# A hybrid decoder trunk: queries, keys and gates by the seven-product form at the front of each mixer, kept in DRAM; other orders behind it

## The chip, the core and the metric

The kernel runs on one core of a Trainium2 chip. The metric is the device time of one execution in microseconds; of several runs the median counts. A core has TensorE (PE) for matrix products into PSUM, VectorE (DVE), ScalarE (ACT) and GpSimd (POOL) for elementwise work, SyncE (SP), which here issues transfers, and 16 DMA engines between DRAM and the core's memory (SBUF). Each engine takes its instructions in the order in which the program gives them, and waits on semaphores for the others.

## The reference, cut to what matters

Two layers over 512 positions of width 1024, one sequence:

```
x = x + 0.5 * swiglu(rms_norm(x, ffn1_norm[l]), ...)             # 1024 -> 2*2816 -> 1024
h = rms_norm(x, mix_norm[l])
proj = h @ w_in[l]
q, k, v, z, xbc, dt_raw, gate_sb, gate_ssm = split(proj)          # 512,512,512,1536,3584,24,1024,1024
y_sb = stick_breaking_attention(q, k, v) @ w_branch_sb[l]         # 4 heads x 128
y_ssm = mamba2_mixer(z, xbc, dt_raw, ...) @ w_branch_ssm[l]       # 8 groups, 24 heads x 64, state 128
merged = sigmoid(gate_sb) * y_sb + sigmoid(gate_ssm) * y_ssm
x = x + merged @ w_out[l]
x = x + 0.5 * swiglu(rms_norm(x, ffn2_norm[l]), ...)
```

The attention weight of a pair (t, s), s < t, is `exp(z - sp + within + cross)`: z is the scaled score, sp = softplus(z), and the other two are sums of -softplus over the positions between s and t. After the last layer comes one more RMSNorm. All is in fp32.

## The kernel before

**Products.** Tokens lie along the free axis (512), channels along the 128 partitions, so h is eight tiles of 128 x 512 ("blocks"). An fp32 product is made of three matmuls on numbers split into a high and a low part in fp32r: hi x hi, hi x lo, lo x hi (`mm3`, L363 to L365). So each operand needs a split first: the high part is a cast on ACT (weights L328, blocks of h L402, other tiles L452 or, with a factor, L454), the low part a subtraction on VectorE (L330, L403, L457, L459). A **plain block** makes 128 output channels: eight blocks of h, 24 matmuls of 512 columns (`dense`, `project`). The **seven** (`seven`, a Strassen form) makes four output blocks, two of each of two kinds, from seven products of 24 matmuls with 256 columns, on sums and differences of the two halves of h and of the weights; its results come in halves of 256 tokens.

**The order of the work.** One thread of Python makes the products in a fixed list; everything else is a generator put into a queue by `spawn(task, wait)`. `dense` calls `tick()` after every block of h (three matmuls), and the seven after every second: each tick takes every task one `yield` further. So `yield 3` is a distance of three ticks in the program, not a time, and the order on every engine is fixed when the program is built. A task that has to wait for another looks once a tick. Weights come in a list of units (L278 issues the load on SP), are split some units ahead, and the loads of DRAM copies and the spills stand in the same queue of SP.

**The norm's factor** `rs` is not known when the mixer begins: the first products are made on unscaled blocks of x times the gain, and the results are multiplied by `rs` afterwards (`scaled`, L593, or L595 with a factor). While that goes on, `scale_blocks` scales the blocks of x; one later product, called with `swap=True`, has the scaled blocks split anew (`swapped`, L402 and L403: the **swap**) for all that follow it.

**A mixer, before.** (1) Two sevens (`four_gates`) make the gates of output blocks 2 to 5, apply tanh and spill them to the DRAM array `gd`. (2) Plain blocks q0, k0 (PSUM tiles `pa`), q1, k1 (with the swap), q2, k2, then v by tokens, q3, k3. Each q and k is split from PSUM or scaled first (`qkv_parts`), and a head's `attention` is spawned after its k, 8 and 9 ticks later for the first two heads. (3) A list of steps (`group_steps`) mixes z, x, b, c blocks (with a four-tap convolution, `conv_block`, L1119 on ACT and three L1122 on VectorE), more gates, and the state-space scan of eight groups (`ssd_group`). Until all heads are done and dt is known, tanh is held back (`opened`), since ACT's table of functions has to be switched once (L222 for exp and ln, L1127 where it comes back). (4) Two branch products of attention, two first halves of the state-space branch products, then for each output block the second half, the merge with the gates, the next first half and the attention branch product two places ahead. (5) The output projection.

**One head's attention** (`attention`): for key blocks j = 3, 2, 1, 0 the scores go into `pa` (128 x 128, 256, 384, 512), then abs, exp, ln on ACT (L1021 to L1023), one instruction on VectorE (L1025), a causal mask on POOL, a split (`state` for the 128-wide term, `xs` for the others), sums of later blocks into `pa` by products with constant matrices (`nones` L1058, `ntri` L1060), exp, and a last split to weights.

## Time and profile before

| | us |
|---|---|
| median of three runs (2545.66 to 2546.43) | 2546.18 |
| the profiled execution | 2546.98 |
| its span, first to last instruction | 2545.3 |
| TensorE busy / VectorE / ACT / POOL | 2534.1 / 1796.7 / 1328.9 / 557.7 |
| TensorE waiting for ones, state, g, wlo | 1.1, 0.6, 0.2, 0.2 |

A row of the timeline has the start in us, the duration, the engine, the line of the kernel, the operation, out<-in by the program's names, shapes, and how many such instructions follow each other; in brackets stand the idle time before it and the engine and line that ended it. Starts of matmuls that follow each other give the pitch; a single duration is longer, since they overlap. Rows of waits give the sum, the count and the longest.

### The profile page before, as it was taken

What the parts mean: (1) busy time and instruction counts of PE and PEld (TensorE: products, weight loads), DVE (VectorE), ACT (ScalarE), POOL (GpSimd) and SP (SyncE); (2) the same over time, 40 slices, a digit from 0 to 9 for tenths busy, and PEclk for the clock granted to TensorE, in tenths of its full rate; (3) what the DMA queues carried; (4) which work ended last, traced back from release to release, by engine and by line L of the source; (5) the groups of instructions that cost most, each with busy time, mean ns of one, the idle gap of its engine ahead of it and who ended that gap; (6) DMA issues with size and microseconds to landing.
All of it is one profiled execution on the core that took longest, in us unless ns stands there. A gap on an engine that the chain in (4) does not pass through costs nothing.

```text
span 2545.3 us, 39422 instructions
## 1 busy us (share of the span) xinstructions
PE 2534.1 (100%) x15536; PEld 2293.7 (90%) x15536; DVE 1796.7 (71%) x2332; ACT 1328.9 (52%) x2193; POOL 557.7 (22%) x656
## 2 busy tenths in 40 slices
PE   9999999999999999999999999999999999999998
PEld 7898998889998889989899999988899988999997
DVE  8585886567765477758896768865777644876766
ACT  6353475666664264435563435656666643643434
POOL 0131300124443001313112222000244420122220
PEclk9999999999999999999999999999999999999999
DMA  4555574232233475656656556622333335755552
GB/s 153 157 155 159 161 199 128 75 120 89 102 100 96 145 211 151 172 151 165 180 126 177 148 166 172 199 98 78 115 102 102 100 105 163 194 142 169 145 163 83
DMA packets 112874, 357.35 MB, mean 140 GB/s; under 512 B 12784, under 2 KB 20400, under 8 KB 112688
## 3 DMA queue, kind: packets, MB, share of 16 engines
q1 hardware_dynamic: 96704, 299.13, 35.5%
q0 software_dynamic: 15120, 55.06, 12.1%
q8 instruction: 122, 2.00, 0.3%
q10 hardware_dynamic: 864, 0.64, 0.1%
q14 instruction: 64, 0.52, 0.1%
HBM read 342.10 MB, written 12.68 MB: 139 GB/s over the span
## 4 chain that ended last, share of the span: by engine, by line
PE 96%; DVE 2%; DMA 1%; issue 1%; ACT 1%; SPq 0%; POOL 0%; DVEq 0%; ACTq 0%; POOLq 0%
PE mm L363 26%; PE mm L364 26%; PE mm L365 26%; PE pa L364 4%; PE pa L363 4%; PE pa L365 4%; PE pa L1275 2%; PE pa L1278 1%; PE pt L1257 1%; PE pt L943 1%; PE pt L1253 1%; DVE wlo L330 1%; PE pa L943 0%; PE pa L1060 0%; DMA s<-in_wflat_dram 0%
## 5 line engine op out<-in xcount | busy, mean ns | idle before, releaser
L328 ACT CAST whi<-wraw 128x1024 fp32r<-128x1024 f32 (+3 forms) x433 | 427.8, 988 | 655.5 <-PE mm L365 438.1
L330 DVE TENSOR_TENSOR wlo<-wraw,whi 128x1024 fp32r<-128x1024 f32 (+3 forms) x433 | 533.3, 1232 | 229.4 <-ACT whi L328 228.6
L363 PE MATMUL mm<-hhi,whi 128*128 128x512 f32 (+1 forms) x1472 | 500.7, 340 | 0.0
L365 PE MATMUL mm<-hlo,whi 128*128 128x512 f32 (+1 forms) x1472 | 494.8, 336 | 0.0
L364 PE MATMUL mm<-hhi,wlo 128*128 128x512 f32 (+1 forms) x1472 | 494.5, 336 | 0.1
L365 PEld LDWEIGHTS mm<-hlo,whi 128*128 128x128 f32 x1472 | 276.0, 188 | 30.2
L363 PE MATMUL mm<-th,whi 128*128 128x256 f32 x1080 | 302.2, 280 | 0.0
L364 PEld LDWEIGHTS mm<-hhi,wlo 128*128 128x128 f32 x1472 | 276.6, 188 | 28.0 <-DVE wlo L330 0.6
L364 PE MATMUL mm<-th,wlo 128*128 128x256 f32 x1080 | 301.7, 279 | 0.2 <-DVE wlo L330 0.2
L365 PE MATMUL mm<-tl,whi 128*128 128x256 f32 x1080 | 301.3, 279 | 0.0
L363 PEld LDWEIGHTS mm<-hhi,whi 128*128 128x128 f32 x1472 | 276.4, 188 | 27.2
L330 DVE TENSOR_TENSOR wlo<-s,whi 128x1024 fp32r<-128x1024 f32 x180 | 257.2, 1441 | 34.0 <-ACT whi L328 30.4
L363 PE MATMUL mm<-act,whi 128*128 128x512 f32 (+1 forms) x710 | 273.9, 386 | 0.0
L364 PE MATMUL mm<-act,wlo 128*128 128x512 f32 (+1 forms) x710 | 273.7, 386 | 0.0
L365 PE MATMUL mm<-act,whi 128*128 128x512 f32 (+1 forms) x710 | 273.7, 385 | 0.0
L662 POOL TENSOR_TENSOR g<-g,rs 128x512 f32<-128x512 f32 x70 | 149.3, 2132 | 483.2 <-DVE g L641 453.7
L290 POOL DMA_DIRECT2D s<-in_wflat_dram x105 | 91.8, 899 | 712.2 <-DMA s<-in_wflat_dram 615.5
L328 ACT CAST whi<-s 128x1024 fp32r<-128x1024 f32 x180 | 188.7, 1048 | 61.2 <-PE mm L365 42.2
L365 PEld LDWEIGHTS mm<-tl,whi 128*128 128x128 f32 x1080 | 202.9, 188 | 0.0
L363 PEld LDWEIGHTS mm<-th,whi 128*128 128x128 f32 x1080 | 202.7, 188 | 0.0
L364 PEld LDWEIGHTS mm<-th,wlo 128*128 128x128 f32 x1080 | 202.2, 187 | 0.4 <-DVE wlo L330 0.4
L725 DVE SCALAR_TENSOR_TENSOR x<-mm,x 128x512 f32<-128x512 f32 x93 | 64.2, 690 | 190.8 <-PE mm L365 190.7
(313 smaller groups left out, 5304.0 us busy)
## 6 DMA issues: line engine op xcount, KB each, us to landing
wraw<-in_wflat_dram SPq DMA_DIRECT2D x321, 512.0 KB, 3.7
s<-in_wflat_dram POOLq DMA_DIRECT2D x105, 512.0 KB, 7.5
s<-in_wflat_dram SPq DMA_DIRECT2D x95, 512.0 KB, 5.2
wraw<-in_wflat_dram SPq DMA_DIRECT2D x88, 384.0 KB, 3.1
cumb<-cum_d SPq DMA_DIRECT2D x16, 768.0 KB, 5.0
xd<-x SPq DMA_DIRECT2D x16, 256.0 KB, 5.4
wraw<-in_wflat_dram SPq DMA_DIRECT2D x16, 256.0 KB, 3.3
x<-xd SPq DMA_DIRECT2D x16, 256.0 KB, 5.4
```

The costliest lines, as they stand in the source:

```text
L290: self.nc.gpsimd.dma_start(raw, self.stored(key[:-1] + (part,)), accum_op=ALU.add)
L328: nc.scalar.copy(hi[:, :n], raw[:, :n])
L330: nc.vector.tensor_tensor(lo[:, :n], raw[:, :n], hi[:, :n].bitcast(F32), op=ALU.subtract)
L363: mm(ps, a[0], b[0], start=start, stop=False, **kw)
L364: mm(ps, a[1], b[0], start=False, stop=False, **kw)
L365: mm(ps, a[0], b[1], start=False, stop=stop, **kw)
L662: eng.tensor_tensor(out, r, self.rs[:, cols].unsqueeze(1).to_broadcast([P, 2, SEQ // 2]), op=ALU.mult)
L725: self.nc.vector.scalar_tensor_tensor(x, pd, 0.5, x, op0=ALU.mult, op1=ALU.add)
L943: self.nc.tensor.transpose(pt[:, cs], src[:, cs], self.ident)
L1253: nc.tensor.matmul(cb, bt[:, span(c)], ct[:, span(c)], start=True, stop=True)
L1257: nc.tensor.matmul(pu, btok[:, c, :], xws[c].rearrange("p h d -> p (h d)"), start=True, stop=True)
L1275: nc.tensor.matmul(near[:, at:at + HD], decs[c][:, i, :], xdts[c][:, i, :], start=True, stop=True)
```

## The change

**At the front** a third seven is made, and the sevens' contents change (`four_blocks`): with j0 = 0 and 2 they make q and k of heads 0, 1 and 2, 3, with j0 = 4 the gates of output blocks 2 and 3. All twelve results are multiplied by `rs` and spilled to DRAM: q and k, in halves, to a new array `qd`, the gates after tanh to `gd`. The plain blocks behind the sevens are now the four gates of output blocks 4 and 5 (`rough_gate`): scaled and spilled without tanh (`rough`), which `finer` applies when they come back for the merge. The swap is in the fourth of them, and v follows at once.

**Attention** takes q and k from `qd` through three `raw` tiles (`reloaded`), and every head's task is spawned before the plain gates, with no distance. The weights' splits wait for the head before (`heads_out`). Its outputs lie in tiles of the block pool `x`, which stays open to the end of the merge.

**State-space groups.** The `y` tile of a group is opened by a task of its own (`direct`); `ssd_on` is released earlier and `y_busy` guards the tile, so that a group follows the one before at another distance; b and c of a group wait for `passed`.

**The merge.** Four first halves (AHEAD) instead of two come before the second halves, and the attention branch product in the loop is one place ahead, not two.

The diff, cut to its core:

```diff
+ROUGH = (4, 5)
+AHEAD = 4
...
-def qkv_order():
-    for h in range(SBH):
-        yield from (("q", h), ("k", h))
-        if h == SBH - 2:
-            for u in range(NT):
-                yield "v", u
+def opening_order():
+    for m in ROUGH:
+        yield from (("gs", m), ("gm", m))
+    for u in range(NT):
+        yield "v", u
...
-        if i + 2 < KB:
-            yield (layer, "bsb", MERGE_ORDER[i + 2]), SBH
+        if 0 < i < KB - 1:
+            yield (layer, "bsb", MERGE_ORDER[i + 1]), SBH
...
-    def four_gates(self, base, m, fp):
-        nc, half = self.nc, SEQ // 2
+    def four_blocks(self, base, fp):
+        nc, half, j0 = self.nc, SEQ // 2, base[-1]
         a, b = slice(0, half), slice(half, SEQ)
-        def squash(src, t, cols, scale):
+        def finish(src, t, cols, scale):
             while self.rs is None:
                 yield 1
             r = self.t(fp, [P, SEQ], "c", bufs=2) if t and cols is a else src
             self.normed_half(nc.vector, r, src, cols)
             yield 2
-            self.tables(False)
-            nc.scalar.activation(r, r, AF.Tanh, scale=scale)
-            yield 4
+            if j0 < SBH:
+                to, at = self.qd, 2 * j0
+            else:
+                to, at = self.gd, 2 * FRONT
+                self.tables(False)
+                nc.scalar.activation(r, r, AF.Tanh, scale=scale)
+                yield 4
             for j in range(2):
-                nc.sync.dma_start(self.gd[2 * (m + j) + t][:, cols], r[:, j * half:(j + 1) * half])
+                nc.sync.dma_start(to[at + 2 * j + t][:, cols], r[:, j * half:(j + 1) * half])
         def take(*how):
-            return lambda src: self.spawn(squash(src, *how))
+            return lambda src: self.spawn(finish(src, *how))
...
-    def qkv_parts(self, t, ps, normed, parts):
-        scale = P ** -0.5 if t == "q" else None
-        if normed:
-            two = self.pair(self.yt, ("yt", "yt"))
-            yield from self.split(two, ps, scale)
-            parts[t] = two
-            return
+    def reloaded(self, t, h, parts):
         r = yield from self.take("raw")
-        yield from self.scaled(r, ps, scale)
-        yield 2
+        self.nc.sync.dma_start(r, self.qd[2 * h + (t == "k")])
+        yield 7
         two = self.pair(self.yt, ("yt", "yt"))
-        yield from self.split(two, r)
+        yield from self.split(two, r, P ** -0.5 if t == "q" else -1.0)
         self.give("raw")
         parts[t] = two
...
+            while self.heads_out < h:
+                yield 1
...
+        self.heads_out = h + 1
         yield 2
-        two = self.pair(self.yo, ("ohi", "olo"))
+        two = self.pair(self.xp, ("x", "x"))
...
+        while kind != "x" and self.passed < i - 2:
+            yield 1
...
-            nc.gpsimd.tensor_tensor(heads(y[:, c, :]), x, wide(par[:, G_D + h0:G_D + h0 + HPG]), op=ALU.mult)
+        def direct(c0):
+            while self.y_busy not in (None, g):
+                yield 1
+            if self.y_busy is None:
+                self.y_busy = g
+                begun.append(self.t(mp, [P, NT, GW], "y", bufs=1))
+            for c in (c0, c0 + 1):
+                nc.gpsimd.tensor_tensor(heads(begun[0][:, c, :]), heads(xs[:, c, :]),
+                                        wide(par[:, G_D + h0:G_D + h0 + HPG]), op=ALU.mult)
+            begun.append(c0)
...
+    def rough(self, ps, r, spill):
+        yield 1
+        yield from self.scaled(r, ps)
+        yield 3
+        self.nc.sync.dma_start(spill, r)
+    def finer(self, *tiles):
+        yield 6
+        for r in tiles:
+            self.nc.scalar.activation(r, r, AF.Tanh, scale=0.5)
+            self.gated[r.name] = True
...
-        front = ExitStack()
-        fp = front.enter_context(tc.tile_pool(name=f"front{layer}", bufs=2, reuse_waits="tile"))
-        four = [self.four_gates((layer, 0, "pair", j), FRONT + j, fp) for j in range(0, EARLY - FRONT, 2)]
-        for part in four:
-            next(part)
-        for part in four:
-            for _ in part:
-                pass
-        self.close_t()
-        self.open_norm(self.x, gain)
-        self.hx = []
-        first = []
-        order = list(qkv_order())
-        for i in range(4):
-            while i == 3 and self.scaled_blocks < KB // 2:
-                self.tick()
-            first.append(self.project(layer, *order[i], swap=i == 3, aside=i < 2))
-        xd, self.xd = self.xd, None
-        front.close()
-        self.xpool.__exit__(None, None, None)
+        self.qd = self.t(self.dr, [2 * SBH, P, SEQ], "qd")
         with ExitStack() as mix:
             enter = mix.enter_context
+            gp = enter(tc.tile_pool(name=f"gates{layer}", bufs=2, reuse_waits="tile"))
+            def rough_gate(i):
+                t, m = order[i]
+                ps, _ = self.project(layer, t, m, swap=i == 3, aside=i < 2)
+                r = self.t(gp, [P, SEQ], t)
+                self.spawn(self.rough(ps, r, self.gd[2 * m + (t == "gm")]))
+            order = list(opening_order())
+            with tc.tile_pool(name=f"front{layer}", bufs=2, reuse_waits="tile") as fp:
+                four = [self.four_blocks((layer, 0, "pair", j), fp) for j in (0, 2, 4)]
+                for part in four[:2]:
+                    next(part)
+                for part in four:
+                    for _ in part:
+                        pass
+                self.close_t()
+                self.open_norm(self.x, gain)
+                self.hx = []
+                rough_gate(0)
+            xd, self.xd = self.xd, None
...
-                for i, (t, h) in enumerate(order):
-                    if t == "v":
-                        if h == 0:
-                            self.by_tokens(self.v_part, SEQ, layer, "v")
-                        continue
-                    ps, normed = first[i] if i < len(first) else self.project(layer, t, h)
-                    self.spawn(self.qkv_parts(t, ps, normed, parts[h]))
-                    if t == "k":
-                        self.spawn(self.attention(h, parts[h]), 8 + h if h < 2 else 0)
+                self.heads_out = 0
+                for h in range(SBH):
+                    for t in ("q", "k"):
+                        self.spawn(self.reloaded(t, h, parts[h]))
+                for h in range(SBH):
+                    self.spawn(self.attention(h, parts[h]))
+                for i in range(1, 4):
+                    while i == 3 and self.scaled_blocks < KB // 2:
+                        self.tick()
+                    rough_gate(i)
+                self.by_tokens(self.v_part, SEQ, layer, "v")
...
+                        if m not in ROUGH:
+                            self.gated[r.name] = True
+                    if m in ROUGH:
+                        self.spawn(self.finer(*gates[m]))
```

The order of the instructions moves with it. At the start of head 0's attention in layer 0, VectorE before (`cumb` is the scratch of the log terms, `state` and `xs` their low parts, `yt` splits of q and k, `wlo` of weights):

```order
L459 SCALAR_TENSOR_TENSOR yt_4261<-mm_4196,yt_4260 128x512
L330 TENSOR_TENSOR wlo_4258<-wraw_4119,whi_4257 128x1024
L1025 SCALAR_TENSOR_TENSOR cumb_4195<-pa_4284,cumb_4195 128x128
L1025 SCALAR_TENSOR_TENSOR cumb_4195<-pa_4291,cumb_4195 128x256
L457 TENSOR_TENSOR yt_4321<-mm_4251,yt_4320 128x512
L330 TENSOR_TENSOR wlo_4316<-wraw_4197,whi_4315 128x1024
L457 TENSOR_TENSOR state_4276<-cumb_4195,state_4275 128x128
L457 TENSOR_TENSOR xs_4278<-cumb_4195,xs_4277 128x256
```

and with the change (`hlo` is the swap, L593 a gate's scaling):

```order
L403 TENSOR_TENSOR hlo_4431<-x_86,hhi_4430 128x512
L1024 SCALAR_TENSOR_TENSOR cumb_4300<-pa_4393,cumb_4300 128x128
L459 SCALAR_TENSOR_TENSOR yt_4415<-raw_4362,yt_4414 128x512
L459 SCALAR_TENSOR_TENSOR yt_4418<-raw_4364,yt_4417 128x512
L459 SCALAR_TENSOR_TENSOR yt_4421<-raw_4366,yt_4420 128x512
L403 TENSOR_TENSOR hlo_4449<-x_87,hhi_4448 128x512
L1024 SCALAR_TENSOR_TENSOR cumb_4300<-pa_4400,cumb_4300 128x256
L593 TENSOR_TENSOR gs_4423<-mm_4350,rs_3669 128x512
L403 TENSOR_TENSOR hlo_4459<-x_88,hhi_4458 128x512
L330 TENSOR_TENSOR wlo_4435<-wraw_4302,whi_4434 128x1024
L403 TENSOR_TENSOR hlo_4469<-x_89,hhi_4468 128x512
L457 TENSOR_TENSOR state_4384<-cumb_4300,state_4383 128x128
```

Ahead of `state` now stand four splits of the swap, three of reloaded q and k, a gate's scaling and one weights' split, where one `yt` and one `wlo` stood behind the log terms. ACT at the same place, with the change, from the first abs of head 0 on:

```order
L1020 ACTIVATE cumb_4300<-pa_4400 128x256
L1021 ACTIVATE cumb_4300<-cumb_4300 128x256
L1022 ACTIVATE cumb_4300<-cumb_4300 128x256
L454 ACTIVATE yt_4414<-raw_4362 128x512
L454 ACTIVATE yt_4417<-raw_4364 128x512
L454 ACTIVATE yt_4420<-raw_4366 128x512
L402 CAST hhi_4430<-x_86 128x512
L328 CAST whi_4434<-wraw_4302 128x1024
L402 CAST hhi_4448<-x_87 128x512
L402 CAST hhi_4458<-x_88 128x512
L452 CAST state_4383<-cumb_4300 128x128
```

The three casts from `raw` stand between the ln and the first cast of the swap. And VectorE where ACT's table has been switched back after the last head, before:

```order
L330 TENSOR_TENSOR wlo_5375<-wraw_5262,whi_5374 128x1024
L1185 SCALAR_TENSOR_TENSOR z_4883<-raw_5393,z_4883 128x384
L1122 SCALAR_TENSOR_TENSOR cv_5385<-mm_5261,conv_4679,cv_5385 128x511
L1122 SCALAR_TENSOR_TENSOR cv_5388<-mm_5310,conv_4679,cv_5388 128x511
L1185 SCALAR_TENSOR_TENSOR z_4894<-raw_5400,z_4894 128x384
L1122 SCALAR_TENSOR_TENSOR cv_5385<-mm_5261,conv_4679,cv_5385 128x510
L1122 SCALAR_TENSOR_TENSOR cv_5388<-mm_5310,conv_4679,cv_5388 128x510
L1185 SCALAR_TENSOR_TENSOR z_4911<-raw_5408,z_4911 128x384
L1122 SCALAR_TENSOR_TENSOR cv_5385<-mm_5261,conv_4679,cv_5385 128x509
```

and with the change:

```order
L1189 SCALAR_TENSOR_TENSOR z_4935<-raw_5571,z_4935 128x384
L1124 SCALAR_TENSOR_TENSOR cv_5563<-mm_5342,conv_4760,cv_5563 128x511
L1124 SCALAR_TENSOR_TENSOR cv_5566<-mm_5405,conv_4760,cv_5566 128x511
L1189 SCALAR_TENSOR_TENSOR z_4948<-raw_5583,z_4948 128x384
L1124 SCALAR_TENSOR_TENSOR cv_5563<-mm_5342,conv_4760,cv_5563 128x510
L1124 SCALAR_TENSOR_TENSOR cv_5566<-mm_5405,conv_4760,cv_5566 128x510
L330 TENSOR_TENSOR wlo_5580<-wraw_5452,whi_5579 128x1024
L1189 SCALAR_TENSOR_TENSOR z_4971<-raw_5591,z_4971 128x384
L1124 SCALAR_TENSOR_TENSOR cv_5563<-mm_5342,conv_4760,cv_5563 128x509
```

The weights' split stood ahead of the first tap and is now behind the second pair of taps; a split of z leads. Between the last matmul of head 3 and the first that reuses the tile of the first of these two convolution blocks stood 57 matmuls of 512 columns and seven transposes on TensorE, and now 39 and seven.

## The prediction

> **What bounds the kernel now.** The page comes first: its busy times and, below them, the chain that ended last, by engine.

> ```profile
> span 2545.3 us, 39422 instructions
> PE 2534.1 (100%) x15536; PEld 2293.7 (90%) x15536; DVE 1796.7 (71%) x2332; ACT 1328.9 (52%) x2193; POOL 557.7 (22%) x656
> PE 96%; DVE 2%; DMA 1%; issue 1%; ACT 1%; SPq 0%; POOL 0%; DVEq 0%; ACTq 0%; POOLq 0%
> ```

> TensorE is the bound: 2534.1 of 2545.3 us, and no other engine is above 71%. So the time moves in two ways only: by TensorE's own work, and by stretches in which it stands still. How much standing still there is to win shows in the waits of TensorE (us in total, times, longest).

> ```profile
> PE pt L1566 <- DVE ones L518: 1.1, 1, 1.1
> PE pa L1058 <- DVE state L457: 0.6, 2, 0.3
> PE pt L773 <- ACT g L760: 0.2, 1, 0.2
> PE mm L364 <- DVE wlo L330: 0.2, 1, 0.2
> ```

> About 2 us in the whole program. Little can be gained, and every new wait counts in full. The second row matters: twice, once in each layer, TensorE waits for VectorE at the first weights of head 0.

> **TensorE's work: three sevens for two.** The starts of matmuls give the cost of the two forms, a plain block (24 matmuls of 512 columns) and a product of the seven (24 of 256):

> ```profile
> 390.92 0.40 PE L363 MATMUL pa<-hhi,whi 128*128 128x512 f32 x1
> 401.85 0.39 PE L363 MATMUL mm<-hhi,whi 128*128 128x512 f32 x1
> 365.48 0.28 PE L363 MATMUL pa<-th,whi 128*128 128x256 f32 x1
> 368.31 0.28 PE L363 MATMUL mm<-th,whi 128*128 128x256 f32 x1
> ```

> Between the first two starts lie two plain blocks: 10.93 us, 5.465 a block, 0.2277 a matmul. Between the last two lies one product: 2.83. A seven is 7 x 2.83 = 19.8 us, the four plain blocks that it stands for 21.9. Each layer makes one more block-of-four that way: 2 x 2.06 = **4.1 us less**. All else on TensorE is only reordered. The new casts, tanh and transfers lie beside TensorE's work wherever it does not wait for them: ACT has 48% free over the span and VectorE 29%. Without that cover the 16 reloads cost their two splits each, some 1.2 us.

> **Place A: the first head's attention meets the swap.** "Swap" is the moment at which the eight blocks of h are split again from their scaled values (one ACT and one VectorE instruction each). Before, two plain blocks stood between it and attention; now the three engines do both at once, and the order shows what stands ahead of `state`, the low part of head 0's first log term, for which TensorE waits. Before, in the same stretch:

> ```profile
> 428.59 0.50 PE L363 MATMUL mm<-whi,hhi 128*128 128x512 f32 x1
> 428.92 0.40 PE L364 MATMUL mm<-whi,hlo 128*128 128x512 f32 x1
> 429.39 0.22 PE L1058 MATMUL pa<-state,nones 128*128 128x128 f32 x1
> 429.92 0.33 PE L1058 MATMUL pa<-state,nones 128*128 128x128 f32 x1 [0.31 <-DVE state L457]
> 430.65 0.44 PE L363 MATMUL mm<-whi,hhi 128*128 128x512 f32 x1
> ```

> From 428.59 to 430.65 TensorE starts three matmuls of 512 columns (0.68) and six small ones (about 0.6): 0.8 us are lost a layer. The pieces' durations, on VectorE and then ACT:

> ```profile
> 411.28 1.22 DVE L330 TENSOR_TENSOR wlo<-wraw,whi 128x1024 fp32r<-128x1024 f32 x1
> 412.41 3.09 DVE L403 TENSOR_TENSOR hlo<-x,hhi 128x512 fp32r<-128x512 f32 x5
> 415.42 0.68 DVE L595 SCALAR_TENSOR_TENSOR raw<-pa,rs 128x512 f32<-128x512 f32 x1
> 418.35 1.89 DVE L457 TENSOR_TENSOR yt<-raw,yt 128x512 fp32r<-128x512 f32 x3
> 429.58 0.29 DVE L457 TENSOR_TENSOR state<-cumb,state 128x128 fp32r<-128x128 f32 x1
> 429.78 0.42 DVE L457 TENSOR_TENSOR xs<-cumb,xs 128x256 fp32r<-128x256 f32 x1
> 409.42 3.90 ACT L402 CAST hhi<-x 128x512 fp32r<-128x512 f32 x7
> 425.12 0.37 ACT L1021 ACTIVATE cumb<-pa 128x256 f32<-128x256 f32 x1
> 425.97 0.42 ACT L1023 ACTIVATE cumb<-cumb 128x256 f32<-128x256 f32 x1
> ```

> So a 512-column split takes VectorE 0.60 (five from 412.41 to 415.42) and a weights' split 1.13. Zero is the end of head 0's second score, 256 columns wide. From there TensorE has 27 matmuls of 512 columns before it needs `state`: 6.15 us. ACT needs a hand-over of about 0.2, then abs, exp and ln (425.12 to 426.39: 1.27), then by the new order three casts of reloaded queries and keys (0.6 each, 1.8) and one of the swap (0.56): 3.85. Only then can VectorE go on with `hlo`, and before `state` stand in its order: four `hlo` splits (2.4), two log terms (0.6 together), three `yt` splits (1.8), a gate's scaling (0.6), a weights' split (1.13), and `state` itself (0.29): 6.83. It is done at 10.7; **TensorE stands for 4.5**. Behind `state` come one more `hlo` (0.60) and `xs` (0.42), while TensorE has two small matmuls: 0.75 more. The next scores wait for an exp that stands behind a weights' cast on ACT; I take 0.6 (between 0 and one such cast, about 1), and 0.1 for refilling the pipeline (428.59 to 428.92 is 0.33 instead of 0.23). Sum 6.0; the bounds are 4.4 (the first wait alone) and 6.9 (the second cast in full, longer hand-overs).

> **Place B: the table switch after the last head.** ACT switches tables and catches up on the held tanh; VectorE starts the convolution taps of two blocks whose PSUM tiles TensorE wants back. Before:

> ```profile
> 535.48 0.28 PE L365 MATMUL pt<-dec,yt 128*128 128x128 f32 x1
> 549.37 0.39 PE L363 MATMUL mm<-hhi,whi 128*128 128x512 f32 x1
> 535.79 0.59 ACT L452 CAST ohi<-pt 128x512 fp32r<-128x512 f32 x1 [3.70 <-PE pt L365]
> 536.40 1.28 ACT L1127 ACT_TABLE_LOAD   x1
> 538.76 1.14 ACT L1127 ACTIVATE raw<-cv 128x512 f32<-128x512 f32 x2
> 541.25 1.44 ACT L1119 ACTIVATE cv<-mm,conv 128x512 f32<-128x512 f32 x2
> 542.59 1.76 ACT L1183 ACTIVATE raw<-z 128x384 f32<-128x384 f32 x4
> 543.14 0.56 DVE L1185 SCALAR_TENSOR_TENSOR z<-raw,z 128x384 f32<-128x384 f32 x1 [0.53 <-ACT raw L1183]
> 543.62 1.40 DVE L1122 SCALAR_TENSOR_TENSOR cv<-mm,conv,cv 128x511 f32<-128x511 f32 x2
> 544.93 0.55 DVE L1185 SCALAR_TENSOR_TENSOR z<-raw,z 128x384 f32<-128x384 f32 x1
> ```

> TensorE had 13.8 us of work (57 matmuls and seven transposes) between the head's last matmul and the one that reuses the tile: enough. Now the order has 39 matmuls and the transposes there: 39 x 0.2277 + 0.76 = 9.64. The chain against it: hand-over and cast 0.8, table 1.3, six held tanh at 0.53 (3.2, one more than before), two tap starts 1.34, the tanh of z 0.55: 7.18; then on VectorE by the new order z 0.48, two taps 1.31, z 0.47, two taps 1.31, a weights' split 1.13 (it stood ahead of the taps before, where VectorE was idle), z 0.47, and the third tap 0.74: 5.9. It ends at 13.1: **TensorE stands for 3.5**, 3.6 with the refill. Bounds: 2.9 (a tanh at 0.5, the tap's end overlapped) and 4.1 (one more hand-over of 0.2 at each of three changes of engine).

> Further on, in the first convolution blocks of group 1, an `xs` copy on ACT now stands behind held tanh, a weights' cast and a tap start just ahead of transposes: between 0 and 1.0; I take 0.4.

> **The sum.** A layer: 6.0 + 3.6 + 0.4 - 0.8 = 9.2. Two layers: +18.4. With -4.1: **+14.3**. The profiled execution took 2546.98 us (span 2545.3 and 1.7 around it), 0.8 above the median of the runs shown; 2546.98 + 14.3 = 2561.3, or **2560.5** on the median's footing. By the bounds a layer adds between 6.5 and 11.2: 2555 to 2564.5.

> What I cost at nothing: the spread of the state-space groups, the four leading first halves and the moved branch products. In the new order the values that TensorE needs there are ready, counted by the durations above, before it comes; the spills and reloads are queued on SP before weights that are used three or four units later, some 5 us each, while such a load lands in about 4:

> ```profile
> wraw<-in_wflat_dram SPq DMA_DIRECT2D x321, 512.0 KB, 3.7
> gs<-gd SPq DMA_DIRECT2D x12, 256.0 KB, 2.7
> ```

> Behind a reload that waits for a `raw` tile at place A stand only loads for the value blocks. If that cover is too short, the reload's 2.7 us is late in each layer.

> [...] The opening shows what standing still may cost beyond itself:

> ```profile
> 1.11 4.20 PE L1566 MATMUL pt<-ones 128*128 128x128 f32 x20 [1.11 <-DVE ones L518]
> 544.50 0.49 PE L943 MATMUL pt<-ident,bT 128*128 128x128 f32 x3
> 544.82 0.60 PE L943 MATMUL pt<-ident,cv 128*128 128x128 f32 x4
> ```

> At the start a 128-column matmul takes 0.21 (4.20 for 20), in full run 0.107 (0.32 for three): 2.1 us lost on the first 4.2. If a wait of 3.5 to 4.5 us put TensorE back into that slow pace, each of the four would cost 2.1 more. [...]

> **The rivals.**
> 1. *Only one of the two places stalls* (17%): the orders put it in the other engine's shadow, for example because at place B the held tanh run while TensorE still waits for ACT earlier. A alone: 2 x (6.0 + 0.4 - 0.8) - 4.1 = +7.1, 2553; B alone: 2 x (3.6 + 0.4) - 4.1 = +3.9, 2550. For it: place B has two steps whose handing over I only bound. Against: both chains are made of in-order instructions with durations that hardly vary.
> 2. *The elementwise work runs faster than its rows* (7%, the case of not slower): if ACT and VectorE did A's and B's instructions in half the time where their sources lie in SBUF, A would shrink to about 1.6 and B to about 0.5, and the sum to 2 x (2.1 - 0.8) - 4.1 = -1.5: 2544.7. It decides from VectorE chains of 2.3 us at A instead of 6.8. Against it: 412.41 and 418.35 are the same SBUF operands, at 0.60 each.
> 3. *The slow pace after the long waits* (12%): 4 x 2.1 = 8.4 on top: 2569. [...]
> 4. *A late transfer* (8%): 2 x 2.7 to 2 x 3.7 on top: 2566 to 2568. Against it: before loses nothing to a transfer within the layers.
> 5. My forecast, both stalls as summed: 56%, its own range 2555 to 2565.

> **How the numbers follow.** A measurement of this kernel tells no change from about 0.2%, 5.1 us: 2541.1 to 2551.3. Faster than that needs the 4.1 and more, with a gain that I have not seen: 4%. Within it: rival 2's rest and B alone, 12%. Slower: 84%. The range leaves out most of rival 2 and the upper half of rival 3: 2548 to 2569.

> **What would show it.** In the trace after: a wait of TensorE on VectorE's `state` (the `nones` matmul) of 4 to 5 us in each layer, followed by one on `xs` below 1; a wait of the first matmul of a new `mm` tile on VectorE's tap of about 3.5 after the table load; three sevens at 19.8 each. I am wrong if `state` waits under 2 us, if the sevens cost more than 20 us, if 128-column matmuls behind a long wait start at 0.21 intervals, or if waits on transfers appear.

## The result, and the profile after

The changed kernel takes 2569.08 us (median of five runs, 2568.64 to 2570.37) against 2546.18 (2545.66 to 2546.43): a ratio of 1.0091, 95% interval 1.0077 to 1.0106. It is slower by 22.9 us, in the direction forecast, but 8.6 us above the forecast of 2560.5 and 0.08 us above the range. 2569 was the figure of the third rival, the slow pace after the long waits. The profiled execution took 2569.03.

The page of the changed kernel, its span, busy times and, by engine, the chain of work that ended last:

```profile
span 2567.3 us, 39845 instructions
PE 2539.7 (99%) x15680; PEld 2303.0 (90%) x15680; DVE 1822.1 (71%) x2356; ACT 1339.1 (52%) x2207; POOL 562.4 (22%) x660
PE 95%; DVE 2%; ACT 1%; issue 1%; DMA 1%; POOL 0%; SPq 0%; DVEq 0%; POOLq 0%; ACTq 0%
```

TensorE's waits in it (us in total, times, longest):

```profile
PE mm L363 <- DVE cv L1124: 6.7, 2, 3.3
PE pa L1057 <- DVE state L457: 5.5, 2, 2.7
PE pa L1057 <- DVE cumb L1024: 2.3, 2, 1.2
PE mm L363 <- ACT z L1184: 1.6, 2, 0.8
```

The first row is place B, the second and third are place A, the fourth is a wait on z that I had not counted. Each is there twice, once a layer. TensorE's timeline at the three places of layer 0 (start, duration, instruction):

```profile
432.87 0.39 PE L365 MATMUL mm<-hlo,whi 128*128 128x512 f32 x1
434.42 0.30 PE L1057 MATMUL pa<-state,nones 128*128 128x128 f32 x1 [1.16 <-DVE cumb L1024]
437.46 0.47 PE L1057 MATMUL pa<-state,nones 128*128 128x128 f32 x1 [2.75 <-DVE state L457]
...
440.06 0.63 PE L365 MATMUL mm<-wlo,hhi 128*128 128x512 f32 x1
440.48 0.63 PE L363 MATMUL mm<-whi,hhi 128*128 128x512 f32 x1
...
442.54 0.40 PE L365 MATMUL mm<-wlo,hhi 128*128 128x512 f32 x1
442.78 0.40 PE L363 MATMUL mm<-whi,hhi 128*128 128x512 f32 x1
...
562.42 0.77 PE L363 MATMUL mm<-hhi,whi 128*128 128x512 f32 x1 [3.35 <-DVE cv L1124]
...
563.41 0.63 PE L365 MATMUL mm<-hlo,whi 128*128 128x512 f32 x1
563.84 0.63 PE L363 MATMUL mm<-hhi,whi 128*128 128x512 f32 x1
...
620.78 0.50 PE L363 MATMUL mm<-hhi,whi 128*128 128x512 f32 x1 [0.78 <-ACT z L1184]
```

Behind the waits at A and B a matmul of 512 columns starts 0.42 to 0.43 us after the one before (440.06 to 440.48, 563.41 to 563.84), until about 442.5 and 565.4; then 0.23 to 0.24 again (442.54 to 442.78). Behind the shorter wait on z there is nothing of the kind. The granted clock says it too. In a view by stretches (length, then TensorE's busy time; the clock granted to it, PEclk, is the third last), the 15 us around A and three parts of them:

```profile
430.00:445.00 15.00, 10.95 (x40) 8.49 (x39) 14.00 (x26) 9.15 (x20) 1.37 (x4) 0.77 0.31 101
432.20:435.61 3.41, 1.35 (x6) 0.74 (x4) 3.41 (x7) 1.97 (x6) 0.29 (x1) 1.00 0.52 154
435.61:439.02 3.41, 1.42 (x5) 1.12 (x6) 3.34 (x8) 0.50 (x1) 0.00 (x0) 0.50 0.57 184
439.02:442.44 3.42, 3.42 (x10) 2.74 (x10) 3.03 (x6) 3.41 (x7) 0.00 (x0) 0.50 0.07 30
```

In layer 0 the trace has TensorE's clock at half from 435.61 to 442.44, so from within the wait on, and at B from 561.90 to 565.32; everywhere else in the layer it is 1.00, from 5.5 us on, where this record begins.

**Where the time went.** Taking from each interval between starts the pitch of its width, the intervals above that lose, by place and layer: A 7.0 and 8.0 us, B 4.9 and 5.2, z 1.0 and 1.0; together 27.1. Of these about 18.5 are the waits themselves (4.7 and 4.9 at A, 3.5 at B, 0.94 at z) and 8.5 the starts at half pace. The same pitches summed over all matmuls fall by 4.0: that is what the sevens bring. With before's own 1.6 at A gone, 27.1 - 1.6 - 4.0 = 21.5 of the 22.05 between the two profiled executions.

### The profile page after: what moved, and what is told of

Same layout as the page of the kernel before. It is cut to its first block, busy times and chain, and to the rows that moved or that the text cites. A ratio compares the mean times of both kernels' runs of the same rounds, so it can differ in the third digit from the quotient of the medians.

```text
span 2567.3 us, 39845 instructions
## 1 busy us (share of the span) xinstructions
PE 2539.7 (99%) x15680; PEld 2303.0 (90%) x15680; DVE 1822.1 (71%) x2356; ACT 1339.1 (52%) x2207; POOL 562.4 (22%) x660
## 4 chain that ended last, share of the span: by engine, by line
PE 95%; DVE 2%; ACT 1%; issue 1%; DMA 1%; POOL 0%; SPq 0%; DVEq 0%; POOLq 0%; ACTq 0%
PE mm L363 26%; PE mm L364 26%; PE mm L365 26%; PE pa L364 4%; PE pa L363 4%; PE pa L365 4%; PE pa L1288 2%; PE pa L1291 1%; PE pt L1270 1%; PE pt L1266 1%; PE pt L947 1%; DVE wlo L330 1%; PE pa L1059 0%; PE pa L947 0%; DMA s<-in_wflat_dram 0%
## 5 line engine op out<-in xcount | busy, mean ns | idle before, releaser
L330 DVE TENSOR_TENSOR wlo<-wraw,whi 128x1024 fp32r<-128x1024 f32 (+3 forms) x431 | 532.6, 1236 | 224.2 <-ACT whi L328 223.5
L363 PE MATMUL mm<-hhi,whi 128*128 128x256 f32 (+1 forms) x1440 | 486.7, 338 | 8.2 <-DVE cv L1124 6.7
L365 PE MATMUL mm<-hlo,whi 128*128 128x256 f32 (+1 forms) x1440 | 479.8, 333 | 0.0
L364 PE MATMUL mm<-hhi,wlo 128*128 128x256 f32 (+1 forms) x1440 | 479.4, 333 | 0.0
L363 PE MATMUL mm<-th,whi 128*128 128x256 f32 x1128 | 315.5, 280 | 0.0
L364 PE MATMUL mm<-th,wlo 128*128 128x256 f32 x1128 | 315.1, 279 | 0.2 <-DVE wlo L330 0.2
L365 PE MATMUL mm<-tl,whi 128*128 128x256 f32 x1128 | 314.7, 279 | 0.0
L363 PEld LDWEIGHTS mm<-hhi,whi 128*128 128x128 f32 x1440 | 271.1, 188 | 34.4 <-issue 7.1
L365 PEld LDWEIGHTS mm<-hlo,whi 128*128 128x128 f32 x1440 | 270.7, 188 | 28.1
L330 DVE TENSOR_TENSOR wlo<-s,whi 128x1024 fp32r<-128x1024 f32 x188 | 266.9, 1431 | 40.3 <-ACT whi L328 36.7
L364 PEld LDWEIGHTS mm<-hhi,wlo 128*128 128x128 f32 x1440 | 271.4, 188 | 25.2
L363 PE MATMUL mm<-act,whi 128*128 128x512 f32 (+1 forms) x710 | 273.9, 386 | 0.0
L364 PE MATMUL mm<-act,wlo 128*128 128x512 f32 (+1 forms) x710 | 273.7, 386 | 0.0
L365 PE MATMUL mm<-act,whi 128*128 128x512 f32 (+1 forms) x710 | 273.7, 385 | 0.0
L365 PEld LDWEIGHTS mm<-tl,whi 128*128 128x128 f32 x1128 | 211.8, 188 | 0.0
L363 PEld LDWEIGHTS mm<-th,whi 128*128 128x128 f32 x1128 | 211.8, 188 | 0.0
L364 PEld LDWEIGHTS mm<-th,wlo 128*128 128x128 f32 x1128 | 211.2, 187 | 0.4 <-DVE wlo L330 0.4
## 6 DMA issues: line engine op xcount, KB each, us to landing
wraw<-in_wflat_dram SPq DMA_DIRECT2D x319, 512.0 KB, 3.6
s<-in_wflat_dram POOLq DMA_DIRECT2D x109, 512.0 KB, 7.6
s<-in_wflat_dram SPq DMA_DIRECT2D x99, 512.0 KB, 5.1
xd<-x SPq DMA_DIRECT2D x16, 256.0 KB, 6.6
raw<-qd SPq DMA_DIRECT2D x16, 256.0 KB, 4.0
wraw<-in_wflat_dram SPq DMA_DIRECT2D x16, 256.0 KB, 3.1
```

Source lines behind the costliest of these rows:

```text
L330: nc.vector.tensor_tensor(lo[:, :n], raw[:, :n], hi[:, :n].bitcast(F32), op=ALU.subtract)
L363: mm(ps, a[0], b[0], start=start, stop=False, **kw)
L364: mm(ps, a[1], b[0], start=False, stop=False, **kw)
L365: mm(ps, a[0], b[1], start=False, stop=stop, **kw)
```

## The experiments

All times are medians beside runs of the kernel before on the same chip (2546.1 to 2546.3).

**Keep TensorE busy in the waits** (e1): products whose results nobody reads, in `weights` (place A) and at the head of `project` (place B). Theory: TensorE falls to half pace after a long stop. Rival: the matmuls behind the wait start late because their own operands come late, one after the other; at A, where the swap feeds them, that was plausible.

```diff
             for part in behind.get(j, ()):
+                if h == 0 and j == NT - 2:
+                    junk = self.t(self.ptr, [P, SEQ], "pt")
+                    for _ in range(4 if part is behind[j][0] else 11):
+                        nc.tensor.matmul(junk, self.nones, q[0], start=True, stop=True)
                 nc.tensor.matmul(pz[:, P:n], self.nones, part, start=False, stop=False, skip_group_check=True)
...
+        if key[1:] == ("gm", 1):
+            junk = self.t(self.pa, [P, SEQ], "pa")
+            for _ in range(14):
+                self.nc.tensor.matmul(junk, self.nones, self.h[0][0], start=True, stop=True)
```

> Nothing of the work is left out; TensorE makes matmuls whose results nobody reads while it would stand still: at place A 4 before the first weights product with the high part of the log term and 11 between its high and its low part, at place B 14 before the product that waits for the third tap, each 128x512 at 0.2277 us, some 2.5 to 3.2 us in a wait. Theory 1 (TensorE falls to half pace after a long wait): the waits stay as long in sum, but the matmuls behind them start at 0.23 us and not at 0.43; the slow starts lost 2.2 and 1.4 us in layer 0, 3.2 and 1.6 in layer 1, 8.5 in all, so 2569.1 - 8.5 = 2560.6 (2559 to 2562.5). Theory 2 (the matmuls behind the wait start late since their operands or tiles come late one after the other): no matmul is faster for it, 2569 (2567.5 to 2571).

Measured 2563.16 (2562.45 to 2563.57), ratio 1.0067 (1.0054 to 1.0079). Its TensorE timeline at A, and the same stretch in the view by stretches:

```profile
434.02 2.77 PE L1064 MATMUL pt<-yt,nones 128*128 128x512 f32 x11
436.93 0.33 PE L1065 MATMUL pa<-state,nones 128*128 128x128 f32 x1
...
439.02 0.40 PE L363 MATMUL mm<-whi,hhi 128*128 128x512 f32 x1
439.26 0.39 PE L364 MATMUL mm<-whi,hlo 128*128 128x512 f32 x1
...
442.27 0.50 PE L363 MATMUL pa<-yt,yt 128*128 128x512 f32 x1 [0.34 <-ACT cumb L1071]
```

```profile
430.00:445.00 15.00, 13.85 (x62) 10.51 (x61) 14.09 (x26) 10.29 (x21) 1.37 (x4) 1.00 0.32 102
```

The product with the low part of `state` starts 3.04 us after the one with the high part, as in the changed kernel (434.42 to 437.46): the chain is as long as it was. But the granted clock is 1.00 instead of 0.77, and the matmuls behind start 0.24 apart. The rival is out: the operands were there. The gain is 5.9 us (6.6 between the profiled executions) and not 8.5: 1.0 us (0.5 a layer) came back as a wait of the next scores on ACT's exp, which the slow pace had covered (the last row); the rest lies partly in the refills around the added matmuls (0.3 at B), and I have not settled all of it.

**Take three reloads out of A's chain** (e2).

```diff
     def reloaded(self, t, h, parts):
+        while (t, h) not in (("q", 0), ("k", 0), ("q", 1)) and not self.normed:
+            yield 1
         r = yield from self.take("raw")
```

> Reloads of k1, q2, k2, q3, k3 are held back until the swap is over, so that three casts (1.8 us of ACT) and three splits (1.8 us of VectorE) leave the chain ahead of the low part of the log term at place A. Theory 1 (the chain counted in instructions sets the wait, and half pace follows only a wait near 3.5 us and more): the wait of 4.2 us falls to about 1 to 2, no slow starts behind it; place A loses about 2 a layer instead of 7.5, so 2569.1 - 2 x 5.3 = 2558.5 (2556 to 2561). Theory 2 (half pace follows any wait of some length): the waits fall by 3.6 at most, the slow starts stay: 2569.1 - 7.2 = 2562 (2561 to 2564). If another thing sets the wait, 2567 or more.

Measured 2562.60, with an unusual spread (2560.37 to 2565.91); ratio 1.0067 (1.0055 to 1.0080). By its sum the second theory was right. TensorE's timeline at A in layer 0 and at B in layer 1:

```profile
434.34 0.33 PE L1059 MATMUL pa<-state,nones 128*128 128x128 f32 x1 [1.35 <-DVE state L457]
435.28 0.39 PE L1061 MATMUL pa<-xs,ntri 128*128 128x256 f32 x1 [0.45 <-DVE xs L457]
...
436.76 0.63 PE L364 MATMUL mm<-whi,hlo 128*128 128x512 f32 x1
437.19 0.63 PE L365 MATMUL mm<-wlo,hhi 128*128 128x512 f32 x1
...
1830.88 0.47 PE L363 MATMUL mm<-hhi,whi 128*128 128x512 f32 x1 [3.34 <-DVE cv L1126]
```

and the stretches around the latter (1.79 of the first 3.41 us busy, 1.69 of the second, PEclk third last):

```profile
1825.75:1829.16 3.41, 1.79 (x12) 1.34 (x10) 3.41 (x6) 1.23 (x3) 0.00 (x0) 1.00 0.00 0
1829.16:1832.57 3.41, 1.69 (x7) 1.42 (x8) 3.41 (x7) 1.72 (x3) 0.00 (x0) 1.00 0.45 149
1832.57:1835.98 3.41, 3.41 (x16) 2.82 (x15) 3.03 (x4) 2.03 (x4) 0.00 (x0) 1.00 0.22 50
```

The waits at A fell as counted, from 3.9 to 1.8 us of idle time. But two stops of 1.35 and 0.45 are followed by the half pace all the same, and it begins 1.2 us after the second one; while at B in layer 1 an idle time of 3.34 is followed by none. A sharp length of the stop does not explain both.

**Let the taps go first at B** (e3). The held tanh wait some ticks after the table has been switched back.

```diff
         yield from self.opened()
+        if held:                       # sigma: the held gates
+            yield 5
         self.nc.scalar.activation(r, ps, AF.Tanh, scale=0.5)
...
             yield from self.opened()   # z_part
+            yield 4
             r = yield from self.take("raw")
```

> When the table has been switched back, the held tanh of the gates wait five more ticks and those of z four, so that the tap starts of the two convolution blocks come first at place B. Theory 1 (the counted chain sets the wait, half pace behind it): the wait of 3.4 us and the slow starts behind it go, 5 us a layer, against about 0.7 a layer that group 0 of the state space may then wait for a product on POOL: 2569.1 - 8.7 = 2560.4 (2558.5 to 2562). Theory 2 (no half pace, only the wait goes): 2569.1 - 7.0 + 1.4 = 2563.5. If B only moves on to the next tile: 2567 or more.

Measured 2559.38 (2559.05 to 2561.29), ratio 1.0054 (1.0041 to 1.0067), inside the range of theory 1 (2558.5 to 2562). The wait on the tap is gone from the list; in its place stands one on a product of POOL in group 0, 0.9 us a layer:

```profile
PE pt L1271 <- POOL xw L1237: 1.8, 2, 0.9
```

**Both edits** (e4).

> Both edits together, reloads held and the held tanh staggered. Theory 1: the gains add up, 2569.1 - 10.6 - 8.7 = 2549.8 (2547 to 2553), with about 2 us a layer still lost at place A; the wait on z in the second pair of groups (0.9 a layer) stays. If the two stalls hide further waits of the new order: 2555 or more.

Measured 2556.88 (2554.53 to 2558.25), ratio 1.0040 (1.0027 to 1.0054): 7 us above the forecast, since I had taken the half pace at A for gone and the next sums for ready. In the profile A still loses about 2.1 a layer in waits and 1.6 in half pace behind them, and further on the next sums wait some 1.3 us more:

```profile
PE pa L1059 <- DVE state L457: 2.7, 2, 1.4
...
```

**Waits of set lengths** (e5), put into the kernel before, to price the half pace by itself.

```diff
+    def pause(self, fp):               # ahead of the 3rd, 5th, 7th down product of two slices
+        nc = self.nc
+        b = self.t(fp, [P, P], "late", F32R, bufs=1)
+        junk = self.t(self.ptr, [P, SEQ], "pt")
+        nc.tensor.matmul(junk[:, :P], self.nones, self.nones, start=True, stop=True)
+        nc.scalar.copy(b, junk[:, :P])
+        for _ in range(next(self.pauses)):
+            nc.scalar.activation(b, b.bitcast(F32), AF.Copy, scale=0.5)
+        nc.tensor.matmul(junk[:, P:2 * P], self.nones, b, start=True, stop=True)
...
+                        if s < 2 and i in (2, 4, 6):
+                            self.pause(fp)
```

> The kernel before, with 24 waits of TensorE put into the down projections of both feed-forward parts of both layers (ahead of the third, fifth and seventh product of the first two slices): a small product, a chain of 3 to 15 ACT copies, and a small product that needs its end; nobody reads the results. At about 0.3 us a copy the waits are some 0.8 to 4.5 us long, three of each length in mixed order, 60 to 70 us in all. Theory 1 (half pace follows a wait from a sharp length on, between the 0.9 us that did nothing and the 1.35 + 0.45 that did): the three waits of a length behave alike. Theory 2 (a window that runs on by itself decides, so that the phase counts): waits of the same middle length are followed by slow matmuls in some places and not in others, and the slow starts last between 0 and 7 us. By either the time is 2610 to 2660.

Measured 2636.07 (ratio 1.0359, 1.0345 to 1.0373). Two pauses of the same length in its TensorE timeline:

```profile
233.20 0.33 PE L549 MATMUL pt<-late,nones 128*128 128x128 f32 x1 [1.77 <-ACT late L548]
...
233.87 0.40 PE L366 MATMUL mm<-act,whi 128*128 128x512 f32 x1
234.11 0.40 PE L364 MATMUL mm<-act,whi 128*128 128x512 f32 x1
...
2516.44 0.33 PE L549 MATMUL pt<-late,nones 128*128 128x128 f32 x1 [1.77 <-ACT late L548]
...
2517.40 0.63 PE L366 MATMUL mm<-act,whi 128*128 128x512 f32 x1
2517.83 0.63 PE L364 MATMUL mm<-act,whi 128*128 128x512 f32 x1
```

The trace also records from when to when the clock is at half. Each such stretch, but the one at the program's end, is 3.41 us long, or twice that, and in each of five traces (the changed kernel, e2 to e5) they start whole multiples of 3.4133 us apart, to within 4 ns; in e5 there are twelve. For counting I continue these starts through each trace in steps of 3.4133 us and call them marks, and the time from one to the next a window. Two of the three pauses with 2.46 us of idle time, by such windows:

```profile
100.14:103.55 3.41, 1.48 (x7) 1.27 (x8) 0.70 (x2) 2.66 (x7) 0.00 (x0) 1.00 0.42 154
103.55:106.96 3.41, 3.41 (x10) 2.66 (x9) 0.67 (x1) 0.00 (x0) 0.00 (x0) 0.50 0.00 0
...
2363.18:2366.59 3.41, 2.38 (x12) 1.77 (x10) 0.69 (x1) 0.87 (x3) 0.00 (x0) 1.00 1.02 303
2366.59:2370.00 3.41, 1.98 (x9) 1.70 (x10) 1.06 (x1) 2.19 (x6) 0.87 (x1) 1.00 0.23 95
2370.00:2373.41 3.41, 3.41 (x16) 2.83 (x16) 0.16 (x1) 0.00 (x0) 0.00 (x0) 1.00 0.88 154
```

The first left TensorE idle for 1.94 us of one window, and the next window ran at half the clock. The second was split by a mark, 1.03 us on one side and 1.43 on the other, and nothing followed.

All 24 by the length of the pause:

| idle time of TensorE, us | followed by half pace | lost by it, us |
|---|---|---|
| 0.70, 1.09, 1.43 | 0 of 9 | 0 |
| 1.77 | 1 of 3 | 1.66 |
| 2.46 | 2 of 3 | 1.56 to 1.60 |
| 3.08 to 3.14, 3.77, 4.84 | 9 of 9 | 1.56 to 1.65, once 2.85 |

One window at half pace is seven to nine matmuls of 512 columns at 0.43 and costs 1.6; once there were two windows in a row, fourteen matmuls. It begins up to 1.4 us after the wait. So the second theory described these pauses better: the three of 1.77 us did not behave alike, nor did those of 2.46, and of the two shown the one that lay in a single window was followed by half clock and the one split by a mark was not.

Counted by windows, in the five traces but for their last 25 us, all 18 windows at full clock with 1.94 us of idle time or more were followed by half clock, none with 1.62 or less was, and of the eight from 1.68 to 1.87 five were. Between 1.62 and 1.94 the traces give no sharp limit: in e2 the stops of 1.35 and 0.45 us lie in one window, with 1.68 us of idle time in layer 0 and 1.79 in layer 1, and half clock followed; the 3.34 us at B in layer 1 are split by a mark into windows with 1.62 and 1.72, and it did not. Full clock came back after the half-rate windows with at most 0.17 us of idle time (22 of 22), and not after those with 0.58 or more (5 of 5); of two between, in the changed kernel, it came back after the one with 0.52 and not after the one with 0.44. At place A of the changed kernel, in layer 0, the window up to 435.61 has 2.06 us of idle time and the next is at half; that one has 1.99, and the one after it is at half too.

**The swap earlier, attention later** (e6), on top of e4, to clear A. Here the fourth plain gate, made from swapped blocks, is multiplied by the norm's factor a second time; the instruction is of the same size.

```diff
-                    while i == 3 and self.scaled_blocks < KB // 2:
+                    while i == 2 and self.scaled_blocks < KB // 2:
...
-                ps, _ = self.project(layer, t, m, swap=i == 3, aside=i < 2)
+                ps, _ = self.project(layer, t, m, swap=i == 2, aside=i < 2)
...
-        yield 4 if h == 0 else 2
+        yield 8 if h == 0 else 2
```

> The two edits of the run before, with the swap in the third plain gate instead of the fourth, and head 0's attention four ticks later (8 for 4), so that the swap is over when its log terms come. Theory (the two places, their waits and the half pace behind them are the whole loss): nothing is left at place A and B; before's time 2546.1 - 4.1 for the sevens - 1.2 for before's own stall at the first weights, + 1.8 for the wait on a product of POOL in group 0 (0.9 a layer) + 1.9 for the wait on z (0.94 a layer) = 2544.5 (2543 to 2547). Rival (the reloads and spills or the closer groups cost something else that the long waits hid): 2549 or more.

Measured 2546.93 (2546.65 to 2548.39), ratio 1.0003 (0.9994 to 1.0012): at the upper end of the theory's range. A and B are gone from the list of waits, and with them 22 us. The same kernel with the fourth gate copied instead (e9):

> The same kernel without the two last edits, that is the kernel with the swap in the third gate, its fourth gate copied instead of multiplied by the norm's factor a second time. One VectorE instruction is another of the same size: 2546.9 as before (2546.3 to 2547.8).

It took 2547.34 (ratio 1.0004, 0.9995 to 1.0013). What it still waits for:

```profile
PE pt L1273 <- POOL xw L1239: 1.8, 2, 0.9
PE mm L363 <- ACT z L1186: 1.5, 2, 0.8
...
```

**The merge's old order** (e7), on top of e6: two first halves lead, the attention branch product two places ahead.

```diff
-AHEAD = 4
+AHEAD = 2
...
-                    if 0 < i < KB - 1:
-                        branch_sb(MERGE_ORDER[i + 1])
+                    if i + 2 < KB:
+                        branch_sb(MERGE_ORDER[i + 2])
```

> The kernel of the run before with the merge's order as it was before the change: two first halves lead instead of four, and the attention branch product is two places ahead. If the merge's new order costs and brings nothing, as the prediction had it: the same within 0.5 us. If it hides a wait: slower by 1 us or more; if it makes one: faster by as much.

Measured 2547.14 (2545.94 to 2547.96) beside 2546.93: no difference. On top of e6 this part of the change neither costs nor brings anything.

**The last two waits** (e8), on top of e9.

```diff
             pt = self.transposed(dst)
-            yield 1
+            if p:
+                yield 1
...
-            if c < 2:
-                weighted(c)
+            if c == 0:
+                weighted(0)
+                if g == 0:
+                    weighted(1)
+            elif c == 1 and not (g == 0):
+                weighted(1)
```

> The swap in the third plain gate with the later attention, held reloads and staggered tanh, and two edits against the last two waits: the copies of x to token order are issued one tick earlier for the first pair of groups, and in group 0 the two products on POOL that TensorE needs first come ahead of a mask that waits for ACT. The fourth plain gate, which is made after the swap, is copied instead of multiplied by the norm's factor. Theory (what was left of the loss are those two waits, 1.07 + 0.15 a layer on POOL and 0.94 a layer on z): 2546.93 - 2.4 - 1.9 = 2542.6 (2541.5 to 2544.5, with up to 0.9 a layer of small waits that the new order may have further on); faster than before by the 4.1 us of the sevens at most. Rival (the waits only move on): 2546 or more.

Measured 2545.65 (2545.33 to 2546.54), ratio 0.9998 (0.9989 to 1.0007): between the theory and the rival. The wait on POOL is gone and the one on z down to 0.25, but others stand in their place, further on in the groups:

```profile
PE pt L1274 <- DVE dec L1288: 1.8, 2, 0.9
...
PE pa L947 <- DVE raw L1380: 1.1, 2, 0.5
PE mm L363 <- ACT z L1187: 0.5, 2, 0.3
```

By the starts they cost 1.1, 0.7 and 0.4 a layer, 4.4 in all: what the sevens bring. No version here is faster than the kernel before by more than the interval. Whether the groups' closer spacing is the cause of these waits is not shown: no run here changes the spacing alone.

## Why the prediction was right and wrong

- **The bound** (TensorE, every new wait counts in full): right. 27.1 us lost at three places, less 1.6 and 4.0, make the difference.
- **Three sevens for two, -4.1**: right, 4.0.
- **Place A, 6.0 a layer** (bounds 4.4 to 6.9): the wait for `state` was 4.5 by the count and came to 4.4 (432.87 + 0.23 to 437.46). The chain is there as the orders gave it, the swap's first cast after the three from `raw`, and VectorE's run from the first `hlo` to `state` 6.9 long where 6.83 were counted:

```profile
428.35 1.66 ACT L454 ACTIVATE yt<-raw 128x512 fp32r<-128x512 f32 x3
429.91 0.60 ACT L402 CAST hhi<-x 128x512 fp32r<-128x512 f32 x1
430.54 0.69 DVE L403 TENSOR_TENSOR hlo<-x,hhi 128x512 fp32r<-128x512 f32 x1 [6.46 <-PE mm L365]
437.13 0.28 DVE L457 TENSOR_TENSOR state<-cumb,state 128x128 fp32r<-128x128 f32 x1
```

  The two smaller terms behind it, 0.75 for `xs` and 0.6 for the next scores, came to about 0.4 and nothing in layer 0, where TensorE was slow by then, and to 0.66 and nothing in layer 1, where half clock began only within the wait for `xs`; at full pace (e1) they are 0.65 and 0.5. In all A waits 4.7 and 4.9 a layer, within the bounds.
- **Place B, 3.6** (2.9 to 4.1): right, 3.5.
- **The `xs` copy, 0.4**: did not come. In its stead z cost 0.94, which belongs to what I costed at nothing, the groups' spread: the copy of the first z of the next pair waits for POOL to have read the tile for the earlier group.

```profile
620.25 0.48 ACT L1184 COPY z<-mm 128x384 f32<-128x384 f32 x1 [2.32 <-POOL y L1310]
```

  The rest of that item held: the merge's order is worth nothing (e7), and no transfer is late.
- **The sum +14.3: wrong, and this is the step that failed.** The waits themselves were right to 1.5 us in 18.4 (16.9 net of before's own). What the sum left out is the half pace behind them, 8.5 us. I had it, priced from the opening row at 4 x 2.1 = 8.4, and set it aside as a rival of 12%. But the same pace came behind waits in the middle of dense work: in e5 pauses with 3.08 us of idle time or more were followed by it 9 times in 9, and in the changed kernel all four long waits were. With a row that showed the pace, and two waits a layer of 3.5 to 4.5 us in the sum, it belonged in the sum. That 8.4 came so near 8.5 is partly luck: the four cost 2.2 and 1.4 us in layer 0 and 3.2 and 1.6 in layer 1, by one or two windows each. The range then ended at the rival's bare figure, without its spread, and missed by 0.08 us.
- **Rivals**: one stall only, faster elementwise work and late transfers did not happen. (The sign given for rival 2, a VectorE chain of 2.3 us, does not follow from half durations, which make 3.4; at 6.9 measured it changes nothing.) Rival 3 did, with its size.

## What to carry to other kernels

Where TensorE is the bound and the order is fixed, the wait that makes a stall can be counted from the orders and the durations of a trace to within a few tenths; then ask for each stall what TensorE's pace is behind it, and put that into the sum: here it cost 8.5 us behind four stalls. In e5 no pause of up to 1.43 us was followed by half pace and every one from 3.08 us on was; between them, and where two stops stood close together as in e2, the length of a stop did not tell. A chain of small instructions that one engine does in order (here a swap, reloads and a gate's scaling ahead of one short split) is cheaply mended by moving its links by a few ticks or a block: the four such moves of e6 (reloads held, tanh staggered, swap one gate earlier, attention four ticks later) gave back 22 us together. A saving of 4 us in the bounding engine's work was spent here by three waits of 0.4 to 1.1 us in each layer (e8), so the waits of the new order decide whether a faster form pays.

## What the runs showed of the hardware

The marks lie at other places in each of these traces: the first, counted from the first instruction, at 2.12 us in the changed kernel, 3.03 in e2 and 1.16 in e5. The waits at A, counted alike in the changed kernel and in e3, lost 7.0 and 8.0 us in the one and 7.6 and 7.0 in the other. The runs of e2 differ by 5.5 us, with a mean granted clock of 0.998 in the fastest and 0.996 in the slowest, beside 0.8 us in the first five of before; that the places of the marks make this spread is not shown. And in e1 the half pace had hidden a wait: taking away the slow starts gave back 5.9 us of 8.5, and 1.0 came back as a wait on ACT's exp.
